# The last projection of an encoder layer: seven block products in place of eight

## Chip, cores and metric

The kernel runs on one core of one Trainium2 chip. The metric is the device time of one launch in microseconds (us); before the change it is 895.59 us, the median of three runs from 895.43 to 895.75.

## What is computed

One layer of an encoder over two groups of 256 tokens with the same weights: a token mixer (retention and latent attention), a residual and a norm, then a gated network of width 2816, a second residual and a norm. The model width is 1024 and everything is float32. What matters here is the last part, cut from the reference:

```python
a, bgate = jnp.split(h @ w_up, 2, axis=-1)
a = _dwconv3(a, conv_w, conv_b)
y = (jax.nn.gelu(a, approximate=False) * bgate) @ w_down
x = _layernorm(DEEPNORM_ALPHA * x + (1.0 + g2) * y) * ln2_g + ln2_b
```

`w_down` is 2816 x 1024. The product `@ w_down` over all 512 tokens, with the residual and norm behind it, is what the change touches. Below, g is what stands left of `@ w_down`.

## The kernel before

**Precision.** A float32 value is held as two parts, hi and lo, in TensorE's 32-bit format. ScalarE (ACT) casts the value to hi (`split_into`, line 148), VectorE (DVE) subtracts hi from the value and writes lo (line 139). A product then costs three matmuls into the same bank, hi by hi, hi by lo and lo by hi (`mm3`, lines 157 to 159). One such matmul takes 128 rows of the inner dimension, 128 tokens and up to 512 columns.

**Storage.** Chunks of weights go through three kinds of buffer of 128 x 2048, each there twice: raw (filled by a DMA from SyncE, SP, line 187), hi and lo. Other things lie in a pool of 69 tiles of 128 x 512. TensorE's sums lie in eight banks of 128 x 512.

**The gated network.** For each of 22 tiles of 128 inner features (index f), TensorE computes two banks `ps_a` and `ps_b` for all 512 tokens; ACT and DVE make the convolution and the gelu of `ps_a` (`up_act`), DVE multiplies with `ps_b`, and the result, the tile `gT[f]` of 128 features by 512 tokens, is split into hi and lo (`g_h`, `g_l`).

**The projection down.** The loop goes over two halves of 512 output columns (c), over chunks of four row tiles of `w_down` (`down_w`, tiles `wd_r`, `wd_h`, `wd_l`), over the row tiles of a chunk, and over four tiles of 128 tokens. In the second half the products of the last 12 row tiles are held back and done token tile by token tile, and the last token tile is done in two pieces of 256 columns. For each finished piece `finish` multiplies by the gate, adds the residual, and takes `bn_stats`; after the second half of a token tile come the mean and variance (`bn_aggr`), two passes over each half of the columns (lines 1194 and 1197), and the two DMAs of the output rows. The power of -1/2 for the norm is on GpSimd (POOL, line 303). The eight residual tiles `x2` come from a scratch in DRAM by DMAs that POOL issues (line 1156).

**Order.** TensorE (PE) runs in the order in which the code is written. The other engines' orders are set by the build's scheduler; each engine then runs its own list strictly in order, and waits at the head of the list on semaphores. A DMA is issued when its issuing engine reaches it in its list. A buffer of a pool is taken again when its last readers are done.

## Time and profile before

| of the profiled execution | |
|---|---|
| span | 893.5 us |
| median of the runs | 895.59 us |
| TensorE busy | 877.2 us, 98% of the span, 4485 matmuls |
| DVE busy | 570.4 us, 64% |
| ACT busy | 354.3 us, 40% |
| POOL busy | 49.8 us, 6% |
| first and last matmul of the projection down start | 764.7 us, 885.4 us |
| mean granted TensorE clock | 0.994 |

The profile is of one execution, whose span runs from its first to its last instruction; 2.1 us of the median lie outside it (895.59 - 893.5). "Busy" of TensorE counts a matmul's whole passage, and passages overlap, so a matmul's cost is the distance from start to start of consecutive ones, not its duration. A row of a group reads: line, engine, operation, out<-in, shapes, count, then busy microseconds, mean nanoseconds of one, and the idle time of the engine before them with what ended it. In a row of the timeline the first number is the start and the second the duration, in us; in a row of a table of windows, the stretch, its length, then each engine's busy time (and number of instructions), the granted TensorE clock, the DMA share and GB/s.

### The profile page before, as it was taken

What the parts mean: (1) busy time and instruction counts of PE and PEld (TensorE: products, weight loads), DVE (VectorE), ACT (ScalarE), POOL (GpSimd) and SP (SyncE); (2) the same over time, 40 slices, a digit from 0 to 9 for tenths busy, and PEclk for the clock granted to TensorE, in tenths of its full rate; (3) what the DMA queues carried; (4) which work ended last, traced back from release to release, by engine and by line L of the source; (5) the groups of instructions that cost most, each with busy time, mean ns of one, the idle gap of its engine ahead of it and who ended that gap; (6) DMA issues with size and microseconds to landing.
All of it is one profiled execution on the core that took longest, in us unless ns stands there. A gap on an engine that the chain in (4) does not pass through costs nothing.

```text
span 893.5 us, 11463 instructions
## 1 busy us (share of the span) xinstructions
PE 877.2 (98%) x4485; PEld 736.5 (82%) x4485; DVE 570.4 (64%) x950; ACT 354.3 (40%) x585; POOL 49.8 (6%) x78
## 2 busy tenths in 40 slices
PE   8999999999999999999998999999999999999996
PEld 5778788888889898988886899888888888888885
DVE  5475877684677777885974966447755755323456
ACT  3555766562343443353342166333333343212200
POOL 3030000000000001000020200000000000100001
PEclk9999999999999999999998999999999999999999
DMA  9922212233545425344356323234334533622401
GB/s 302 388 83 60 70 57 92 67 123 95 153 142 182 113 95 153 131 169 161 111 185 206 111 95 94 60 106 153 119 100 137 160 102 122 208 81 93 142 23 71
DMA packets 118374, 114.29 MB, mean 128 GB/s; under 512 B 6853, under 2 KB 97187, under 8 KB 118320
## 3 DMA queue, kind: packets, MB, share of 16 engines
q1 hardware_dynamic: 114688, 104.00, 35.4%
q0 software_dynamic: 2912, 8.45, 3.3%
...
## 4 chain that ended last, share of the span: by engine, by line
PE 94%; DMA 2%; DVE 1%; ACT 1%; issue 0%; SPq 0%; DVEq 0%; ACTq 0%
PE ps_b L157 5%; PE ps_d L157 5%; PE ps_b L159 5%; PE ps_d L159 5%; PE ps_b L158 5%; PE ps_d L158 4%; PE ps_a L158 4%; PE ps_a L159 4%; PE ps_a L157 4%; PE ps_rv L159 2%; PE ps_rv L158 2%; PE ps_rv L157 2%; PE ps_gb L157 2%; PE ps_ga L157 2%; PE ps_ga L159 2%; PE ps_ga L158 2%
## 5 line engine op out<-in xcount | busy, mean ns | idle before, releaser
L484 DVE SCALAR_TENSOR_TENSOR acc<-araw,csil,acc 128x512 f32<-128x512 f32 x112 | 78.3, 746 | 8.1 <-DMA araw<-in_w_ada_dram 8.1
L157 PE MATMUL ps_b<-h_h,wup_h 128*128 128x512 f32 (+1 forms) x200 | 72.9, 364 | 0.3 <-ACT h2m L394 0.3
L158 PE MATMUL ps_a<-h_l,wup_h 128*128 128x512 f32 (+1 forms) x200 | 73.0, 365 | 0.1
L157 PE MATMUL ps_a<-h_h,wup_h 128*128 128x512 f32 (+1 forms) x200 | 72.8, 364 | 0.0
L159 PE MATMUL ps_b<-h_h,wup_l 128*128 128x512 f32 (+1 forms) x200 | 72.8, 364 | 0.0
L158 PE MATMUL ps_b<-h_l,wup_h 128*128 128x512 f32 (+1 forms) x200 | 72.8, 364 | 0.0
L159 PE MATMUL ps_a<-h_h,wup_l 128*128 128x512 f32 (+1 forms) x200 | 72.8, 364 | 0.0
L158 PE MATMUL ps_d<-wd_l,g_h 128*128 128x512 f32 (+1 forms) x198 | 72.5, 366 | 0.0
L157 PE MATMUL ps_d<-wd_h,g_h 128*128 128x512 f32 (+1 forms) x198 | 72.5, 366 | 0.0
L159 PE MATMUL ps_d<-wd_h,g_l 128*128 128x512 f32 (+1 forms) x198 | 72.4, 366 | 0.0
L148 ACT CAST wup_h<-wup_r 128x1024 fp32r<-128x1024 f32 (+1 forms) x46 | 44.3, 1013 | 49.7 <-PE ps_b L158 36.7
L139 DVE TENSOR_TENSOR wd_l<-wd_r,wd_h 128x1024 fp32r<-128x1024 f32 (+1 forms) x24 | 26.2, 1132 | 58.6 <-ACT wd_h L148 58.4
L139 DVE TENSOR_TENSOR wup_l<-wup_r,wup_h 128x1024 fp32r<-128x1024 f32 (+1 forms) x46 | 52.2, 1174 | 11.3 <-ACT wup_h L148 9.5
L148 ACT CAST wd_h<-wd_r 128x1024 fp32r<-128x1024 f32 (+1 forms) x24 | 22.2, 979 | 73.4 <-PE ps_d L159 69.1
L142 DVE TENSOR_TENSOR conv<-conv,ps_b 128x512 f32<-128x512 f32 x22 | 15.1, 687 | 56.7 <-PE ps_b L159 53.6
L157 PEld LDWEIGHTS ps_b<-h_h,wup_h 128*128 128x128 f32 x200 | 37.8, 189 | 6.4 <-ACT h2m L394 0.5
L158 PEld LDWEIGHTS ps_a<-h_l,wup_h 128*128 128x128 f32 x200 | 37.8, 189 | 6.3 <-DVE h_l L139 0.3
L158 PEld LDWEIGHTS ps_b<-h_l,wup_h 128*128 128x128 f32 x200 | 37.7, 189 | 5.9
L157 PEld LDWEIGHTS ps_a<-h_h,wup_h 128*128 128x128 f32 x200 | 37.7, 189 | 5.9
L159 PEld LDWEIGHTS ps_a<-h_h,wup_l 128*128 128x128 f32 x200 | 37.8, 189 | 5.9
L159 PEld LDWEIGHTS ps_b<-h_h,wup_l 128*128 128x128 f32 x200 | 37.8, 189 | 5.9
L158 PEld LDWEIGHTS ps_d<-wd_l,g_h 128*128 128x128 f32 x198 | 37.4, 189 | 6.1
...
## 6 DMA issues: line engine op xcount, KB each, us to landing
...
araw<-in_w_ada_dram SPq DMA_DIRECT2D x64, 256.0 KB, 5.4
wd_r<-in_w_down_dram SPq DMA_DIRECT2D x10, 1024.0 KB, 4.8
wada<-in_w_ada_dram SPq DMA_DIRECT2D x32, 256.0 KB, 6.0
wga_r<-in_w_in_dram SPq DMA_DIRECT2D x4, 1024.0 KB, 5.0
wmo_r<-in_w_mla_o_dram SPq DMA_DIRECT2D x4, 1024.0 KB, 4.6
...
wrv_r<-in_w_in_dram SPq DMA_DIRECT2D x4, 1024.0 KB, 5.5
```

Of the source, the lines that this page charges most:

```text
L139: (eng or dve).tensor_tensor(out=out, in0=a, in1=b, op=ALU.subtract)
L142: (eng or dve).tensor_tensor(out=out, in0=a, in1=b, op=ALU.mult)
L148: act.copy(hi, src)
L157: pe.matmul(out, l[0], r[0], start=start, stop=False)
L158: pe.matmul(out, l[0], r[1], start=False, stop=False)
L159: pe.matmul(out, l[1], r[0], start=False, stop=stop)
L484: dve.scalar_tensor_tensor(out=acc[g], in0=raw, scalar=s, in1=acc[g], op0=ALU.mult, op1=ALU.add)
```

## The change

The product is cut into blocks: 2 blocks of 256 tokens (the two groups), 2 blocks of 1408 inner features (11 row tiles each), and 2 blocks of 512 columns. The usual scheme takes eight block products; the change takes seven, with sums of blocks on both sides (Strassen's scheme, one level). In the order of the code they are numbered 1, 2, 5, 3, 6, 7, 4. Each is 11 row tiles by two token tiles (s = 0, 1) of 512 columns, three matmuls each, in chunks of 4, 4 and 3 row tiles, and in a chunk all row tiles of s = 0 stand before those of s = 1. Products 1 and 2 share a pair of banks, so do 5 and 3, and so do 7 and 4: product 2 is summed onto product 1 after ACT has copied product 1 out (tiles `dv`; `dw` is the same copy of product 5), and 4 onto 7 after DVE has added 7 to `dw` (in `finish`).

Sums of weights: products 1, 5, 6 and 4 take theirs from 11 tiles `chain_w` (named `wdx` in the rows below), loaded once by SP; after each split of such a tile a DMA from POOL adds the next block of `w_down` to it in place (`accum_op=ALU.add`, line 1218), 33 times 256 KB in all. Products 2, 3 and 7 take raw blocks through the weight buffers (tiles `wdb`); product 7's get a second block added by POOL DMAs in the same way (line 1226: two of 1 MB, one of 0.75 MB). The split parts of the chain are `wdc_h` and `wdc_l`, made 512 columns at a time; those of the blocks are `wdb_h` and `wdb_l`, 1024 at a time.

Sums of g: `gT[f]` stays unsplit. In the gated network the first 11 tiles' first 256 tokens are split for product 1; each of the other 11 tiles brings three subtractions of 128 x 256 on DVE (`g_combine`). In each product the 11 splits of 128 x 256 for the next product are made (`half_split`, ACT and DVE; tiles `ga` and `gs`), in product 1 also 11 more subtractions.

At the end all token tiles are finished in one piece of 512 columns; the two chunks of product 4 that are held back (row tiles 4 to 10) are done for s = 0, then for s = 1.

```diff
-    def mm3(out, l, r, start, stop):
-        pe.matmul(out, l[0], r[0], start=start, stop=False)
...
+    def mm3(out, l, r, start, stop, skip=False):
+        pe.matmul(out, l[0], r[0], start=start, stop=False, skip_group_check=skip)
+        pe.matmul(out, l[0], r[1], start=False, stop=False, skip_group_check=skip)
+        pe.matmul(out, l[1], r[0], start=False, stop=stop, skip_group_check=skip)
...
+        ga11, g_s3 = [], []
+        T1, T2 = slice(0, 256), slice(256, 512)
+        def half_split(src, name, neg=False):
+            w = t512(F32R, name)
+            if neg:
+                act.mul(w[:, T1], src, -1.0)
+                dve.scalar_tensor_tensor(out=w[:, T2], in0=src, scalar=-1.0, in1=as32(w[:, T1]), op0=ALU.mult, op1=ALU.subtract)
+            else:
+                split_into(w[:, T1], w[:, T2], src)
+            return w
+        def g_combine(f):
+            if f < NF2:
+                ga11.append(half_split(gT[f][:, T1], f"ga11_{f}"))
+                return
+            i = f - NF2
+            if i % 2 == 0:
+                g_s3.append(t512(F32, f"gs3_{i}"))
+            lo, hi = gT[i], gT[f]
+            sub(g_s3[i // 2][:, (T1, T2)[i % 2]], lo[:, T2], lo[:, T1])
+            sub(lo[:, T2], lo[:, T2], hi[:, T2])
+            sub(lo[:, T1], lo[:, T1], lo[:, T2])
         def up_act(f, pa, pb):
...
             act.activation(a, a, AF.Gelu)
             mul(a, a, pb)
-            gT[f] = split(a, f"g{f}")
+            gT[f] = a
+            g_combine(f)
...
-        def down_w(c, k0, n, small_tiles=False):
...
-        def finish(t, c, a, b, ps):
...
-        for c in range(2):
...
-            pieces = [(t, 0, 512, ps512(f"ps_d{c}_{t}")) for t in range(4 - c)]
-            if c:
-                pieces += [(3, a, a + 256, ps512(f"ps_d{c}_3_{a}")) for a in (0, 256)]
...
+        def load_x2(t, c):
+            x2[t][c] = t512(F32, f"x2_{t}_{c}")
+            nc.gpsimd.dma_start(x2[t][c], x1d[t * 128:(t + 1) * 128, c * 512:(c + 1) * 512])
+        def stats2(t, c):
+            for m in range(2):
+                n = 2 * c + m
+                dve.bn_stats(out=st2[t][:, 6 * n:6 * n + 6], in_=x2[t][c][:, m * 256:m * 256 + 256])
+        def finish(t, c, ps, more=None):
+            u = t512(F32, f"v{t}_{c}")
+            gate = gates[5, t // 2, c]
+            if more is not None:
+                add(u, more, ps)
+                mul(u, u, gate)
+            else:
+                mul(u, ps, gate)
+            dve.scalar_tensor_tensor(out=x2[t][c], in0=x2[t][c], scalar=ALPHA, in1=u, op0=ALU.mult, op1=ALU.add)
+            stats2(t, c)
+        def norm_out(t):
+            mv = small(2, f"mv2_{t}")
+            dve.bn_aggr(out=mv, in_=st2[t])
+            rs = rstd_of(mv[:, 1:2], LN_EPS, 1, f"ln3_{t}")
+            dst = outs[t // 2][0, (t % 2) * 128:(t % 2) * 128 + 128, :]
+            for cc in range(2):
+                y = x2[t][cc]
+                dve.scalar_tensor_tensor(out=y, in0=y, scalar=mv[:, 0:1], in1=ln2g[cc], op0=ALU.subtract, op1=ALU.mult)
+            for cc in range(2):
+                y = x2[t][cc]
+                dve.scalar_tensor_tensor(out=y, in0=y, scalar=rs, in1=ln2b[cc], op0=ALU.mult, op1=ALU.add)
+                (nc.scalar if cc else nc.sync).dma_start(dst[:, cc * 512:(cc + 1) * 512], y)
+        CHUNKS = [(0, 4), (4, 4), (8, 3)]
+        chain_w = {}
+        def wd_rows(r, c, k0, n=1):
+            return w_down[:, r * NF2 + k0:r * NF2 + k0 + n, c * 512:(c + 1) * 512]
+        def chain_of(more, nxt):
+            def weights(k0, n):
+                hi, lo = w_tiles(f"wdc{k0}")
+                for k in range(k0, k0 + n):
+                    if more is None:
+                        chain_w[k] = t512(F32, f"wdx{k}")
+                        nc.sync.dma_start(chain_w[k], wd_rows(0, 0, k)[:, 0])
+                    cols = slice((k - k0) * 512, (k - k0 + 1) * 512)
+                    split_into(hi[:, cols], lo[:, cols], chain_w[k])
+                    if nxt is not None:
+                        nc.gpsimd.dma_start(chain_w[k], wd_rows(*nxt, k)[:, 0], accum_op=ALU.add)
+                return hi, lo
+            return weights
+        def block_of(r, c, plus=None):
+            def weights(k0, n):
+                raw = w_raw(lambda raw: [(kf(raw, n, 512), wd_rows(r, c, k0, n))], n * 512, f"wdb{r}{c}_{k0}")
+                if plus is not None:
+                    nc.gpsimd.dma_start(kf(raw, n, 512), wd_rows(*plus, k0, n), accum_op=ALU.add)
+                return w_split(raw, n * 512, f"wdb{r}{c}_{k0}")
+            return weights
+        ga = {1: ga11}
+        a_of = {2: lambda i: half_split(gT[NF2 + i][:, T1], f"ga12_{i}"),
+                5: lambda i: half_split(gT[i][:, T2], f"gs1_{i}"),
+                3: lambda i: half_split(gT[NF2 + i][:, T1], f"gs4_{i}"),
+                6: lambda i: half_split(gT[i][:, T1], f"gs2_{i}"),
+                7: lambda i: half_split(g_s3[i // 2][:, (T1, T2)[i % 2]], f"gs3s_{i}"),
+                4: lambda i: half_split(gT[NF2 + i][:, T2], f"ga22_{i}", True)}
+        w_of = {1: chain_of(None, (0, 1)), 2: block_of(1, 0), 5: chain_of(1, (1, 1)), 3: block_of(1, 1),
+                6: chain_of(1, (1, 0)), 7: block_of(1, 1, (0, 1)), 4: chain_of(1, None)}
+        def product(p, nxt, banks, first, last):
+            ga.setdefault(nxt, [])
+            def parts_for_next(k0, n):
+                for i in range(k0, k0 + n) if nxt else ():
+                    ga[nxt].append(a_of[nxt](i))
+                    if nxt == 2:
+                        sub(gT[NF2 + i][:, T1], gT[NF2 + i][:, T1], gT[i][:, T1])
+            def mms(s, k0, n, wc):
+                for k in range(k0, k0 + n):
+                    a = ga[p][k]
+                    mm3(banks[s], (a[:, s * 128:s * 128 + 128], a[:, 256 + s * 128:384 + s * 128]),
+                        cut(wc, slice(None), slice((k - k0) * 512, (k - k0 + 1) * 512)), first and k == 0, k == NF2 - 1, skip=not last or not first)
+            held = []
+            for k0, n in CHUNKS:
+                wc = w_of[p](k0, n)
+                parts_for_next(k0, n)
+                if not nxt and k0:
+                    held.append((k0, n, wc))
+                    for s in range(2):
+                        mms(s, k0, n, wc)
+            if held:
+                for s in range(2):
+                    for h in held:
+                        mms(s, *h)
+                    yield s
+        def banks(name):
+            return [ps512(f"ps_d{name}_{s}") for s in range(2)]
+        b1 = banks(1)
+        drain(product(1, 2, b1, True, False))
+        v = [t512(F32, f"dv{s}") for s in range(2)]
+        for s in range(2):
+            act.copy(v[s], b1[s])
+            load_x2(s, 0)
+        drain(product(2, 5, b1, False, True))
+        for s in range(2):
+            finish(s, 0, b1[s])
+        b5 = banks(5)
+        drain(product(5, 3, b5, True, False))
+        w = [t512(F32, f"dw{s}") for s in range(2)]
+        for s in range(2):
+            act.copy(w[s], b5[s])
+            load_x2(s, 1)
+        drain(product(3, 6, b5, False, True))
+        b6 = banks(6)
+        drain(product(6, 7, b6, True, True))
+        for s in range(2):
+            sub(v[s], b6[s], v[s])
+            add(w[s], v[s], w[s])
+        for s in range(2):
+            finish(s, 1, b5[s], v[s])
+            norm_out(s)
+        for s in range(2):
+            for c in (1, 0):
+                load_x2(2 + s, c)
+        b7 = banks(7)
+        drain(product(7, 4, b7, True, False))
+        for s in range(2):
+            finish(2 + s, 1, b7[s], w[s])
+        for s in range(2):
+            gate = gates[5, 1, 0]
+            mul(v[s], v[s], gate)
+            dve.scalar_tensor_tensor(out=x2[2 + s][0], in0=x2[2 + s][0], scalar=ALPHA, in1=v[s], op0=ALU.mult, op1=ALU.subtract)
+        for s in product(4, None, b7, False, True):
+            u = t512(F32, f"v{2 + s}_0")
+            mul(u, b7[s], gates[5, 1, 0])
+            sub(x2[2 + s][0], x2[2 + s][0], u)
+            stats2(2 + s, 0)
+            norm_out(2 + s)
```

**Order of the instructions at three places.** First DVE from the last tile of the gated network on; `conv_6893` and `conv_6877` are that tile before and in the change. Before:

```order
L1099 SCALAR_TENSOR_TENSOR conv_6893<-ps_a_6843,vecs,conv_6893 128x2x255
L1101 SCALAR_TENSOR_TENSOR conv_6893<-ps_a_6843,vecs,conv_6893 128x2x255
L142 TENSOR_TENSOR conv_6893<-conv_6893,ps_b_6844 128x512
L139 TENSOR_TENSOR wd_4_l<-wd_4_r,wd_4_h 128x1024 x2
L139 TENSOR_TENSOR g_l<-conv_6893,g_h 128x512
L139 TENSOR_TENSOR wd_8_l<-wd_8_r,wd_8_h 128x1024 x2
L139 TENSOR_TENSOR wd_12_l<-wd_12_r,wd_12_h 128x1024 x2
```

In the change the corresponding list, from the third of the subtractions that stand before it to the fourth lo part of product 1's weights (`wdx_6903`, `wdx_6908`, `wdx_6913` and `wdx_6918` are row tiles 0 to 3):

```order
L139 TENSOR_TENSOR conv_6354<-conv_6354,conv_5540 128x256
L139 TENSOR_TENSOR wdc_l<-wdx_6908,wdc_h 128x512
L139 TENSOR_TENSOR ga_4_6985<-conv_6430,ga_4_6985 128x256
L139 TENSOR_TENSOR ga_5_6989<-conv_6507,ga_5_6989 128x256
L142 TENSOR_TENSOR conv_6877<-conv_6877,ps_b_6828 128x512
L139 TENSOR_TENSOR ga_6_6993<-conv_6583,ga_6_6993 128x256
L139 TENSOR_TENSOR ga_7_6997<-conv_6662,ga_7_6997 128x256
L139 TENSOR_TENSOR wdc_l<-wdx_6913,wdc_h 128x512
L139 TENSOR_TENSOR ga_8_7042<-conv_6730,ga_8_7042 128x256
L139 TENSOR_TENSOR conv_6430<-conv_6430,conv_5608 128x256
L139 TENSOR_TENSOR conv_6507<-conv_6507,conv_5676 128x256
L139 TENSOR_TENSOR wdc_l<-wdx_6918,wdc_h 128x512
```

Before, the lo parts of the first chunk stand ahead of this piece and two instructions of 1024 columns follow the multiplication with `ps_b`. Now product 1's lo parts of row tiles 1 to 3 stand between splits of g for product 2 (`ga`) and subtractions.

Second, POOL's list: before, all from the residual tiles on:

```order
L1156 DMA x_0_0_6915<-x1d 128x512
L1156 DMA x_1_0_6917<-x1d 128x512
L1156 DMA x_2_0_6919<-x1d 128x512
L1156 DMA x_3_0_6921<-x1d 128x512
L1156 DMA x_0_1_7257<-x1d 128x512
L1156 DMA x_1_1_7259<-x1d 128x512
L1156 DMA x_2_1_7261<-x1d 128x512
L1156 DMA x_3_1_7263<-x1d 128x512
L303 TENSOR_TENSOR ln_0_rs<-ln_0_ve,half_m 128x1
```

In the change, from the first of product 7's weights on; the rows left out are row tiles 2 to 9 of the same kind:

```order
L1226 DMA wdb_0_r<-in_w_down_dram 128x4x512
L1226 DMA wdb_4_r<-in_w_down_dram 128x4x512
L1218 DMA wdx_6903<-in_w_down_dram 128x512
L1218 DMA wdx_6908<-in_w_down_dram 128x512
...
L1218 DMA wdx_7037<-in_w_down_dram 128x512
L1164 DMA x_2_1_7664<-x1d 128x512
L1164 DMA x_2_0_7666<-x1d 128x512
L1164 DMA x_3_1_7668<-x1d 128x512
L1164 DMA x_3_0_7670<-x1d 128x512
L1226 DMA wdb_8_r<-in_w_down_dram 128x3x512
L303 TENSOR_TENSOR ln_0_rs<-ln_0_ve,half_m 128x1
```

The DMA that adds to product 7's last chunk (`wdb_8`, row tiles 8 to 10) stands behind those for `wdb_0` and `wdb_4`, the eleven that make product 4's weights, and four residual tiles.

Third, DVE where one pair of banks passes to the next product. Before, at the change from the first to the second half of the columns, which have banks of their own:

```order
L139 TENSOR_TENSOR wd_20_l<-wd_20_r,wd_20_h 128x1024
L139 TENSOR_TENSOR wd_0_l<-wd_0_r,wd_0_h 128x1024 x2
L142 TENSOR_TENSOR v_0_0_7237<-ps_d_0_6923,ada_0_0_6221 128x512
L142 TENSOR_TENSOR v_0_0_7242<-ps_d_1_6924,ada_0_0_6221 128x512
L1148 SCALAR_TENSOR_TENSOR x_0_0_6915<-x_0_0_6915,v_0_0_7237 128x512
L142 TENSOR_TENSOR v_0_0_7247<-ps_d_2_6925,ada_0_1_6226 128x512
L1148 SCALAR_TENSOR_TENSOR x_1_0_6917<-x_1_0_6917,v_0_0_7242 128x512
L142 TENSOR_TENSOR v_0_0_7252<-ps_d_3_6926,ada_0_1_6226 128x512
L1151 BN_STATS st_0_6911<-x_0_0_6915 128x6 x2
```

In the change, behind the lo parts of product 7's last chunk; `ps_d_0_7672` is the bank of s = 0 that product 7 leaves to product 4, and the last row is the one that reads it:

```order
L1180 SCALAR_TENSOR_TENSOR x_1_1_7359<-x_1_1_7359,v_1_7646 128x512
L139 TENSOR_TENSOR wdc_l<-wdx_6903,wdc_h 128x512
L1309 SCALAR_TENSOR_TENSOR x_3_0_7670<-x_3_0_7670,dv_7073 128x512
L139 TENSOR_TENSOR wdc_l<-wdx_6908,wdc_h 128x512
L1185 BN_AGGR mv_0_7634<-st_0_6895 128x2
L139 TENSOR_TENSOR wdc_l<-wdx_6913,wdc_h 128x512
L139 TENSOR_TENSOR wdc_l<-wdx_6918,wdc_h 128x512
L1169 BN_STATS st_1_6896<-x_1_1_7359 128x6 x2
L302 TENSOR_SCALAR ln_0_ve<-mv_0_7634 128x1
L1190 SCALAR_TENSOR_TENSOR x_0_0_7075<-x_0_0_7075,mv_0_7634,ln2g_6887 128x512
L1190 SCALAR_TENSOR_TENSOR x_0_1_7356<-x_0_1_7356,mv_0_7634,ln2g_6889 128x512
L145 TENSOR_TENSOR v_1_7800<-dw_7353,ps_d_0_7672 128x512
```

Two residual passes, four lo parts of product 4's weights, the sums of two token tiles and the first two passes of a norm stand ahead of that addition.

55 lines of the change are left out of this document (1 added, 54 removed).

## The prediction

> **What bounds the kernel now.** I read the engine shares first, then the chain of work that ended last, then the projection's own instructions.
>
> ```profile
> PE 877.2 (98%) x4485; PEld 736.5 (82%) x4485; DVE 570.4 (64%) x950; ACT 354.3 (40%) x585; POOL 49.8 (6%) x78
> ...
> PE 94%; DMA 2%; DVE 1%; ACT 1%; issue 0%; SPq 0%; DVEq 0%; ACTq 0%
> ```
>
> TensorE is busy nearly throughout and is 94% of the chain: before the change a matmul saved is time saved. Next the projection down, by windows (the fourth ends with the last matmul) and by two of its three groups of matmuls, then the distance between matmuls on its timeline.
>
> ```profile
> core 0: us, PE busy (x) PEld busy (x) DVE busy (x) ACT busy (x) POOL busy (x), PEclk, DMA share, GB/s
> 764.70:794.90 30.20, 30.20 (x135) 24.98 (x135) 8.37 (x8) 6.54 (x7) 0.35 (x1) 1.00 0.40 132
> ...
> 855.30:885.70 30.40, 30.35 (x168) 26.43 (x166) 17.41 (x35) 0.00 (x0) 2.83 (x3) 1.00 0.14 52
> 885.70:893.50 7.80, 0.00 (x0) 0.00 (x0) 4.33 (x9) 0.00 (x0) 0.98 (x1) 0.79 0.17 67
> sum 128.80, PE 120.95 PEld 102.52 DVE 53.53 ACT 20.75 POOL 4.17; mean PE 24.19 PEld 20.50 DVE 10.71 ACT 4.15 POOL 0.83
> ```
> ```profile
> L157 PE MATMUL ps_d<-wd_h,g_h x198: 277/389/397, 764.7 to 885.1; 128*128 128x512 f32 x154, 128*128 128x256 f32 x44
> ...
> L159 PE MATMUL ps_d<-wd_h,g_l x198: 278/389/390, 765.2 to 885.4; 128*128 128x512 f32 x154, 128*128 128x256 f32 x44
> ```
> ```profile
> 829.63 0.28 PE L159 MATMUL ps_d<-wd_h,g_l 128*128 128x256 f32 x1
> 829.75 0.28 PE L157 MATMUL ps_d<-wd_h,g_h 128*128 128x256 f32 x1
> ...
> 870.74 0.39 PE L157 MATMUL ps_d<-wd_h,g_h 128*128 128x512 f32 x1
> 870.97 0.39 PE L158 MATMUL ps_d<-wd_l,g_h 128*128 128x512 f32 x1
> 871.19 0.39 PE L159 MATMUL ps_d<-wd_h,g_l 128*128 128x512 f32 x1
> 871.42 0.39 PE L157 MATMUL ps_d<-wd_h,g_h 128*128 128x512 f32 x1
> ```
>
> The projection takes 120.95 us of TensorE with no gap, DVE is busy for 53.53 us of it, and 7.8 us follow the last matmul. A 512-wide matmul costs (871.42 - 870.74) / 3 = 0.227 us, a 256-wide one 0.12. There are 3 x 154 = 462 and 3 x 44 = 132: 104.9 + 15.8 = 120.7, as measured.
>
> **TensorE's saving.** Seven products of 11 x 2 x 3 = 66 matmuls are 462 of 512 columns: 104.9 us. That is **-15.8 us**, if it never waits.
>
> **DVE's new work.** Its prices:
>
> ```profile
> L139 DVE TENSOR_TENSOR wd_l<-wd_r,wd_h 128x1024 fp32r<-128x1024 f32 x18 | 21.4, 1222 | 58.5 <-ACT wd_h L148 58.4
> L1194 DVE SCALAR_TENSOR_TENSOR x<-x,mv,ln2g 128x512 f32<-128x512 f32 x8 | 5.6, 744 | 0.0
> L139 DVE TENSOR_TENSOR wd_l<-wd_r,wd_h 128x512 fp32r<-128x512 f32 x4 | 2.5, 684 | 0.0
> ```
> ```profile
> L139 DVE TENSOR_TENSOR h_l<-h2m,h_h 128x256 fp32r<-128x256 f32 x16 | 6.1, 418 | 7.8 <-ACT h_h L395 7.8
> ```
> ```profile
> 880.99 0.74 DVE L1197 SCALAR_TENSOR_TENSOR x<-x,ln_rs,ln2b 128x512 f32<-128x512 f32 x1
> 881.65 0.42 DVE L142 TENSOR_TENSOR v<-ps_d,ada 128x256 f32<-128x256 f32 x1
> 881.99 0.74 DVE L1197 SCALAR_TENSOR_TENSOR x<-x,ln_rs,ln2b 128x512 f32<-128x512 f32 x1
> 882.65 0.42 DVE L1148 SCALAR_TENSOR_TENSOR x<-x,v 128x256 f32<-128x256 f32 x1
> ...
> 885.69 0.42 DVE L142 TENSOR_TENSOR v<-ps_d,ada 128x256 f32<-128x256 f32 x1 [2.16 <-PE ps_d L159]
> 886.14 0.43 DVE L1148 SCALAR_TENSOR_TENSOR x<-x,v 128x256 f32<-128x256 f32 x1
> 886.61 0.43 DVE L1151 BATCH_NORM_STATS2 st<-x 128x6 f32<-128x256 f32 x1
> 887.07 0.26 DVE L1189 BATCH_NORM_AGGREGATE mv<-st 128x2 f32<-128x24 f32 x1
> ```
>
> Independent instructions start 0.08 us before the last one's duration is over (880.99 to 881.65 is 0.66 for 0.74). So in a queue a 1024-wide split costs 1.14, a 512-wide one 0.60, a pass (scalar_tensor_tensor) 0.66, a 256-wide operation 0.34 (a pass of 256, no row of its form, 0.37), `bn_stats` 0.34. During the seven products DVE gets 44 splits of the chain (26.4), three times five of 1024 and one of 512 (18.9), 66 of g (22.8), 11 subtractions (3.7), 20 multiplications and additions of 512 (12.0), 20 passes (13.2), 14 `bn_stats` (4.8) and trifles: about 103 us, **against 104.9 of TensorE**. Twice the 53.5 of before, in a list of fixed order: any place where the order is bad stalls TensorE. I followed the list at each first use:
>
> 1. Product 1's start.
>
> ```profile
> 759.50 0.78 ACT L1097 ACTIVATE conv<-ps_a,vecs 128x512 f32<-128x512 f32 x1 [3.15 <-PE ps_a L159]
> ```
> ```profile
> 760.31 0.75 DVE L1099 SCALAR_TENSOR_TENSOR conv<-ps_a,vecs,conv 128x510 f32<-128x510 f32 x1 [2.43 <-ACT conv L1097]
> 761.09 0.75 DVE L1101 SCALAR_TENSOR_TENSOR conv<-ps_a,vecs,conv 128x510 f32<-128x510 f32 x1
> ```
>
> DVE is through these passes at 761.8. Seven 256-wide operations (2.4) and the lo part of row tile 0 (0.6) end at 764.8, when product 1 begins (764.7 before). Row tile 1's follows in time. Row tile 2's is behind two splits of g, the 512-wide multiplication, two more splits: 0.34 x 4 + 0.60 x 2 = 2.6, done 3.6 us after the start; TensorE gets there at 1.7. Wait 1.9. Row tile 3's needs 3 x 0.34 + 0.6 = 1.6 more, TensorE 0.7. Wait 0.9. Sum **2.9 us**.
>
> 2. Product 7's third chunk. The bank of product 6's s = 0 is complete 9 x 0.227 = 2.0 us before product 7 starts, 0.4 later DVE subtracts. From there its list holds ten 512-wide operations (6.0), three 1024-wide splits (3.4), 11 splits of g with a sign (4.1), two passes (1.3), two `bn_stats` (0.7) and the lo part of row tiles 8 and 9 itself (1.2): 16.7, done 15.1 us into product 7. TensorE wants it after 48 matmuls and one, 11.1. Wait **4.0 us**.
>
> 3. Product 4's first matmul into the bank of s = 0. The addition that frees it stands behind the rows shown last in the section on the change: 7.2 us of DVE after row tiles 8 and 9. TensorE has 17 matmuls left then, 3.9. Wait **3.3 us**.
>
> 4. Row tiles 8 and 9 of product 4: after that addition 9.7 us of DVE, against 36 matmuls and one, 8.4; then 1.3 against 0.7. Wait **1.8 us**.
>
> Together 12.0 us; nothing else on the list comes later than its use. ACT covers its own share (each cast is shorter than the DVE operation that follows it); in the gated network 33 subtractions and 11 splits of 256 columns (15.0) replace 22 lo parts of 512 (13.2), under TensorE's work.
>
> **The tail.** Before, from the last bank: 885.69 to 887.07 is 1.4 us up to `bn_aggr`. Now the multiplication is 512 wide (0.60), a pass of the token tile before it stands next (0.66), then the subtraction (0.72 with its dependence), two `bn_stats` (0.34 + 0.46): 2.8. With 0.1 for the wider last matmul, **+1.5 us**; the rest of the tail stays.
>
> If the accumulating DMAs were free, the sum would be -15.8 + 12.0 + 1.5 = -2.3 us.
>
> **The accumulating DMAs.** The trace has none. Its plain ones:
>
> ```profile
> wd_r<-in_w_down_dram SPq DMA_DIRECT2D x10, 1024.0 KB, 4.8
> ...
> x<-x1d POOLq DMA_DIRECT2D x8, 256.0 KB, 5.2
> ```
> ```profile
> 470.00:474.00 4.00, 4.00 (x19) 3.13 (x17) 0.00 (x0) 0.00 (x0) 0.00 (x0) 1.00 1.04 396
> ```
>
> All engines busy move 396 GB/s. Lower bound: an accumulating DMA as a plain one, since it must at least bring in the block. Upper bound: three plain ones (read the block, read the tile, write the tile). I take twice a plain one: both operands have to be fetched, the writing runs beside the fetching in a plain one too. The Trainium skill ("Collectives: The Full Stack", section "The bandwidth ceiling: the fold count and why AG ≠ RS ≠ AR") gives half the rate for a sum of two sources against a copy, 31 against 62 GB/s, because both sources are read on one ring; no run here shows it, and the sum by it is the one below.
>
> Where does it reach the path? The sums for products 5, 6 and 4 have a product or more of time each. The tight place is POOL's list at product 7: `wdb_0`, `wdb_4`, eleven tiles, four residual tiles, then `wdb_8`. The raw buffer for `wdb_0` is free when product 3's second chunk is split, wanted 44.9 + 2.9 + 5.4 = 53.2 us into the products; its load takes 4.8 and the issue some more, so the first sum starts at 58.5. Up to `wdb_8`'s landing 2 + 2.75 + 0.75 = 5.5 MB are summed (11 MB at twice the price), 1 MB of residuals and 1.75 MB of raw blocks loaded: 13.75 x 1.049 MB at 390 GB/s is 37 us. So 95.5, some 2 us for the landing, 1.05 for the cast: 98.5. Product 7's third chunk is wanted at 5 x 14.97 + 2.9 + 10.9 = 88.7. TensorE waits about 9.5, and 1.0 more for the lo part: 10.5 in place of point 2's 4.0. Points 3 and 4 stay, since DVE waits at the same row. **Sum: -15.8 + 2.9 + 10.5 + 3.3 + 1.8 + 1.5 = +4.2 us.** Against the profiled execution 893.5 + 4.2 = 897.7 of span; the median has 2.1 us more: **899.8 us**.
>
> **Rivals.**
> A. *The sums cost little more than plain DMAs*: up to about 1.55 times, they land before DVE wants them, and the order of DVE decides: 895.6 - 2.3 = **893.3 us**. For it: the DMA share of 0.40 and 0.14 in the projection's first and last window leaves much spare.
> B. *The sums cost three plain ones* (slower still): 16.5 + 2.75 = 19.25 MB, 51.8 us, landing at 112.3 + 1.05; the wait is 25.5 and the sum +19.2: **915 us**. By this reckoning the kernel loses from 1.7 times on, where the wait passes 6.3 us.
> C. *TensorE stays the bound*: DVE's list keeps ahead by some slack that I missed and only the saving and the tail count: 895.6 - 14.3 = **881.3 us**. Against it: DVE's 103 us for 104.9, and instructions that wait at the head of a strict list.
> D. *A long wait also halves TensorE's clock.*
>
> ```profile
> 474.00:477.20 3.20, 0.18 (x1) 0.00 (x0) 0.52 (x1) 1.59 (x3) 0.00 (x0) 1.00 0.15 54
> 477.20:480.30 3.10, 2.44 (x4) 1.12 (x4) 3.10 (x5) 2.48 (x4) 0.00 (x0) 0.50 0.00 0
> 480.30:484.02 3.72, 3.72 (x9) 2.95 (x10) 1.75 (x3) 0.00 (x0) 0.00 (x0) 0.50 0.88 254
> ```
>
> Once, 3.0 us without matmuls were followed by 6.8 us at half clock, worth 3.4 us of full work. After a 10 us wait the same follows; of it DVE's next wait (point 3) hides most, since TensorE would reach that bank 3.3 us early. At most 3.4 more after it: **903 us**. The Trainium skill ("TensorE: Matmul & The Clock Gate", "What's actually happening") puts the window at about 3.4 us of idleness; the trace agrees with its half clock, at 0.50, and shows it after 3.0.
>
> **How the numbers follow.** Forecast (about twice) 0.41, A 0.25, B 0.17, D 0.11, C 0.06. What this kernel's measurement can tell from no change is 0.2%, 1.8 us. Faster by that: C and three quarters of A, 0.25; same: the rest of A and the forecast's lower edge (1.6 to 1.8 times), 0.14; slower 0.61. The likeliest's own range is 896 to 903 (1.75 to 2.2 times). The range to hold 8 in 10 leaves out C and the far half of B: 892 to 915.
>
> **What would show it.** Right: TensorE's longest wait lies before product 7's 49th matmul, ended by ACT's cast of `wdb_8`, itself by a POOL DMA; DVE near 100 us in the products; waits of 2 to 4 us at the start and at the bank of product 4. An accumulating tile of 256 KB then shows a rate near half of 396 GB/s when they queue. Wrong: DVE, not a DMA, ends that wait (A); waits on accumulated tiles at products 5 or 6 as well (B); no waits over 1 us (C). A list of DVE that I mistimed by 2 us would shift the forecast by as much.

## The result and the profile after

The change makes the kernel slower: 901.39 us median (901.32 to 902.67) against 895.67 (895.43 to 896.64), a ratio of 1.0064 with an interval of 1.0050 to 1.0078, or 5.7 us. The forecast was 899.8, in a range from 892 to 915, with slower at 0.61. The profiled execution has a span of 899.6, 6.1 more than before.

The engine shares of after, its chain of waits by engine, and the queue of the DMAs that POOL issues (packets, megabytes, share of 16 DMA engines):

```profile
PE 866.6 (96%) x4353; PEld 722.2 (80%) x4353; DVE 623.4 (69%) x1097; ACT 386.9 (43%) x682; POOL 83.1 (9%) x114
...
q0 software_dynamic: 9120, 19.99, 10.8%
...
PE 87%; DVE 5%; DMA 4%; ACT 2%; issue 1%; SPq 0%; DVEq 0%; ACTq 0%; POOLq 0%
```

The chain was TensorE to 94%; it is now 87%, and DVE, DMAs and ACT have what it lost. TensorE's timeline of after, its first and last matmul of the projection down and three in between:

```profile
765.83 0.39 PE L157 MATMUL ps_d<-wdc_h,ga 128*128 128x512 f32 x1
...
864.95 0.79 PE L157 MATMUL ps_d<-wdb_h,gs3s 128*128 128x512 f32 x1 [10.20 <-ACT wdb_h L148]
...
867.22 0.63 PE L157 MATMUL ps_d<-wdb_h,gs3s 128*128 128x512 f32 x1
867.65 0.63 PE L158 MATMUL ps_d<-wdb_l,gs3s 128*128 128x512 f32 x1
...
889.82 0.39 PE L159 MATMUL ps_d<-wdc_h,ga 128*128 128x512 f32 x1
```

From the first start to the end of the last slot (889.82 + 0.23) are 124.2 us, for 462 matmuls that need 104.9. Most of the 19.3 us between is in four groups of TensorE's waits in the projection (engine, tile and line, what it waited for; us in all, times, longest):

```profile
PE ps_d L157 <- ACT wdb_h L148: 10.2, 1, 10.2
PE ps_d L158 <- DVE wdc_l L139: 3.3, 4, 1.6
PE ps_d L157 <- DVE v L145: 0.5, 1, 0.5
PE ps_d L158 <- DVE wdb_l L139: 0.5, 1, 0.5
```

These are 14.5 us of idleness; the rest is matmuls that restart late or at half clock (867.22 to 867.65 is 0.43 a matmul, against 0.227). The long wait followed back, in the chain of waits of after (start, duration, what):

```profile
842.74 1.15 DVE wdb_l L139
843.90 11.62 DMA wdb_r<-in_w_down_dram
855.58 0.52 issue
856.10 7.65 DMA wdb_r<-in_w_down_dram
...
863.85 1.05 ACT wdb_h L148
```

DVE's split of `wdb_0` frees the raw buffer at 843.9; SP loads the 0.75 MB of `wdb_8` in 11.6 us; only then can POOL issue its sum, which needs 7.7 us; then ACT casts, and TensorE starts at 864.95. The stretches around it, of after (busy time of each engine, granted clock, DMA share, GB/s):

```profile
842.00:853.00 11.00, 11.00 (x50) 9.10 (x49) 11.00 (x20) 5.39 (x13) 4.87 (x7) 1.00 1.11 229
853.00:864.00 11.00, 1.75 (x8) 1.13 (x6) 4.20 (x10) 0.15 (x1) 1.31 (x1) 0.71 0.93 216
864.00:875.00 11.00, 9.04 (x26) 6.59 (x27) 10.07 (x19) 5.68 (x10) 1.00 (x1) 0.67 0.03 9
...
sum 134.90, PE 110.97 PEld 88.67 DVE 106.10 ACT 60.09 POOL 41.20; mean PE 11.10 PEld 8.87 DVE 10.61 ACT 6.01 POOL 4.12
```

While the load and the sum run, the DMA engines are full (1.11 and 0.93) and move 216 to 229 GB/s; the plain row of before had 396 at 1.04. DVE, busy for only 4.2 us from 853 to 864, has 106.1 us of work between 764.7 and the end of the span.

### The profile page after: what moved, and what is told of

Read it like the earlier page. It is cut to its first block, busy times and chain, and to the rows that moved or that the text cites. A ratio compares the mean times of both kernels' runs of the same rounds, so it can differ in the third digit from the quotient of the medians.

```text
span 899.6 us, 11589 instructions
## 1 busy us (share of the span) xinstructions
PE 866.6 (96%) x4353; PEld 722.2 (80%) x4353; DVE 623.4 (69%) x1097; ACT 386.9 (43%) x682; POOL 83.1 (9%) x114
## 3 DMA queue, kind: packets, MB, share of 16 engines
q0 software_dynamic: 9120, 19.99, 10.8%
q10 hardware_dynamic: 720, 1.11, 0.3%
## 4 chain that ended last, share of the span: by engine, by line
PE 87%; DVE 5%; DMA 4%; ACT 2%; issue 1%; SPq 0%; DVEq 0%; ACTq 0%; POOLq 0%
PE ps_a L158 4%; PE ps_a L159 4%; PE ps_a L157 4%; PE ps_b L157 4%; PE ps_b L158 4%; PE ps_b L159 4%; PE ps_d L158 3%; PE ps_d L159 3%; PE ps_d L157 3%; DMA wdb_r<-in_w_down_dram 2%; PE ps_rv L159 2%; PE ps_rv L158 2%; PE ps_rv L157 2%; PE ps_gb L157 2%; PE ps_ga L157 2%; PE ps_ga L158 2%
## 5 line engine op out<-in xcount | busy, mean ns | idle before, releaser
L1124 ACT ACTIVATE conv<-ps_a,vecs 128x512 f32<-128x512 f32 x22 | 17.2, 780 | 71.1 <-PE ps_a L159 71.1
L1218 POOL DMA_DIRECT2D wdx<-in_w_down_dram x33 | 29.5, 1233 | 73.2 <-DVE wdc_l L139 64.4
L159 PE MATMUL ps_rv<-wrv_h,h_l 128*128 128x256 f32 x128 | 36.2, 283 | 0.0
L158 PE MATMUL ps_rv<-wrv_l,h_h 128*128 128x256 f32 x128 | 36.2, 283 | 0.0
L157 PE MATMUL ps_rv<-wrv_h,h_h 128*128 128x256 f32 x128 | 36.2, 283 | 0.0
L1126 DVE SCALAR_TENSOR_TENSOR conv<-ps_a,vecs,conv 128x510 f32<-128x510 f32 x22 | 16.4, 747 | 28.3 <-ACT conv L1124 28.2
```

Of the source, the lines that this page charges most:

```text
L157: pe.matmul(out, l[0], r[0], start=start, stop=False, skip_group_check=skip)
L158: pe.matmul(out, l[0], r[1], start=False, stop=False, skip_group_check=skip)
L159: pe.matmul(out, l[1], r[0], start=False, stop=stop, skip_group_check=skip)
L1124: act.activation(a, pa, AF.Identity, scale=convw[:, 1, f:f + 1], bias=convb[:, f:f + 1])
L1126: dve.scalar_tensor_tensor(out=av_[:, :, 1:256], in0=pv[:, :, 0:255], scalar=convw[:, 0, f:f + 1], in1=av_[:, :, 1:256], op0=ALU.mult, op1 ...
L1218: nc.gpsimd.dma_start(chain_w[k], wd_rows(*nxt, k)[:, 0], accum_op=ALU.add)
```

## The experiments

Each kernel is compared with the kernel before, whose median was 895.5 to 896.1 beside them. The table divides the span of each profiled execution into four, all read from the timeline: the start of the first matmul of the projection down, the stage from there to 0.23 us after the start of the last matmul (its slot; the same is taken for before, where the last one is 256 wide), from there to the end of DVE's last pass, and the closing behind that. The four add up to the span.

| kernel | median us | ratio, interval | first | stage | to DVE's end | closing |
|---|---|---|---|---|---|---|
| before | 895.67 | | 764.7 | 120.9 | 4.6 | 3.3 |
| after | 901.39 | 1.0064, 1.0050 to 1.0078 | 765.8 | 124.2 | 6.2 | 3.3 |
| plain DMAs | 896.50 | 1.0011, 1.0002 to 1.0020 | 765.7 | 117.9 | 6.3 | 5.9 |
| no sums for product 7 | 896.18 | 1.0005, 0.9997 to 1.0014 | 766.0 | 116.0 | 8.0 | 5.7 |
| no sums for product 4 | 895.95 | 1.0007, 0.9998 to 1.0016 | 764.8 | 118.6 | 6.2 | 5.0 |
| TensorE kept busy | 902.45 | 1.0076, 1.0064 to 1.0089 | 765.2 | 124.9 | 6.1 | 3.3 |
| early weights | 898.65 | 1.0039, 1.0027 to 1.0051 | 764.3 | 124.4 | 6.6 | 3.3 |
| own tiles | 896.87 | 1.0015, 1.0006 to 1.0023 | 766.6 | 118.2 | 7.6 | 3.4 |
| both | 895.22 | 1.0000, 0.9989 to 1.0011 | 765.2 | 117.3 | 6.8 | 3.4 |
| both, fewer passes | 894.39 | 0.9988, 0.9979 to 0.9997 | 764.5 | 120.6 | 6.0 | 3.4 |
| plain, fewer passes | 893.04 | 0.9972, 0.9962 to 0.9981 | 764.3 | 114.8 | 6.0 | 5.9 |
| both, lo parts on GpSimd | 895.88 | 1.0001, 0.9991 to 1.0012 | 765.2 | 119.8 | 5.6 | 3.4 |
| light, plain | 885.77 | 0.9889, 0.9876 to 0.9903 | 766.4 | 105.9 | 6.0 | 6.1 |
| light, with sums | 892.71 | 0.9964, 0.9952 to 0.9976 | 765.1 | 117.3 | 6.0 | 3.4 |

Two columns need a word first. "First" varies by 2.3 us among kernels that share everything ahead of it but the position of a few instructions, so the 1.1 us that it is later in after are not shown to be the change's. "Closing" is 3.3 or 3.4 in some kernels and 5.0 to 6.1 in others, and differences of the medians hold that too; it is taken up at the end of this part. What tests the theories is the stage, with two limits. The profiled executions lie from 1.2 us below (TensorE kept busy) to 2.0 us above (both, fewer passes) the median of their kernel, so a difference of stages under some 2 us says little by itself. And DVE's list is that of after, instruction for instruction, only with plain DMAs and without the sums for product 4; in the other kernels the scheduler orders it anew in places.

**What the accumulating DMAs cost.** The first kernel takes the adding away and keeps every DMA; the next two leave out some of the sums whole.

```diff
-                        nc.gpsimd.dma_start(chain_w[k], wd_rows(*nxt, k)[:, 0], accum_op=ALU.add)
+                        nc.gpsimd.dma_start(chain_w[k], wd_rows(*nxt, k)[:, 0])
...
-                    nc.gpsimd.dma_start(kf(raw, n, 512), wd_rows(*plus, k0, n), accum_op=ALU.add)
+                    nc.gpsimd.dma_start(kf(raw, n, 512), wd_rows(*plus, k0, n))
```

> All 36 accumulating DMAs become plain ones of the same size, at the same places of every engine's list; left out is the adding, so the tiles hold the last block alone. Theory (the sums cost about twice a plain DMA and this decides product 7's last chunk): TensorE's wait there falls from 10.7 us to the 3 to 4 us that VectorE's list alone asks for, full clock stays or is lost only briefly, and the time falls from 901.4 to 893 to 895 us. Rival (the two transfers in series, load and then sum, are too late at any price): the wait stays at 7 us or more, the time at 898 or above.

The queue's share and the issues (KB each, median us to landing), first of plain DMAs, then of after:

```profile
q0 software_dynamic: 6304, 19.99, 7.1%
...
wdx<-in_w_down_dram POOLq DMA_DIRECT2D x33, 256.0 KB, 3.7
...
wdb_r<-in_w_down_dram POOLq DMA_DIRECT2D x1, 768.0 KB, 4.5
```
```profile
wdx<-in_w_down_dram POOLq DMA_DIRECT2D x33, 256.0 KB, 7.2
...
wdb_r<-in_w_down_dram POOLq DMA_DIRECT2D x1, 768.0 KB, 7.6
```

Both move 19.99 MB; the queue's other DMAs, those of before, have 3.3%. So the additions make a DMA (10.8 - 3.3) / (7.1 - 3.3) = **1.97 times** as long for the DMA engines: the forecast took 2. The shares of the other kernels with all additions (10.8 to 11.0%) and with plain DMAs alone (7.1 to 7.4%) put it between 1.8 and 2.0. The Trainium skill ("Collectives: The Full Stack", section "The bandwidth ceiling: the fold count and why AG ≠ RS ≠ AR") gives half the rate for a sum of two sources; the trace agrees, at 1.97. On TensorE, timeline, waits and windows of plain DMAs, and last the first window of after:

```profile
765.69 0.39 PE L157 MATMUL ps_d<-wdc_h,ga 128*128 128x512 f32 x1
...
883.34 0.39 PE L159 MATMUL ps_d<-wdc_h,ga 128*128 128x512 f32 x1
```
```profile
PE ps_d L158 <- DVE wdb_l L139: 3.2, 1, 3.2
PE ps_d L157 <- ACT wdc_h L148: 1.3, 1, 1.3
```
```profile
764.70:782.00 17.30, 15.07 (x58) 11.27 (x57) 13.55 (x31) 6.91 (x15) 6.95 (x13) 0.90 0.74 244
...
853.00:864.00 11.00, 7.81 (x28) 5.85 (x27) 11.00 (x24) 3.65 (x6) 0.00 (x0) 0.84 0.13 52
864.00:875.00 11.00, 9.71 (x43) 7.72 (x42) 11.00 (x23) 3.84 (x7) 1.92 (x2) 1.00 0.13 49
```
```profile
764.70:782.00 17.30, 15.09 (x64) 11.51 (x63) 14.51 (x32) 8.52 (x17) 10.74 (x13) 1.00 1.01 196
```

The long wait is gone and 3.2 us for DVE's lo part stand at its place, with DVE busy for 22.00 of 22 us. The stage is 6.3 us shorter and the closing 2.6 longer; the median falls by 4.9 us and misses what was expected by 1.5. Without the longer closing it would be 893.9, an estimate, and within it. The stage, 117.9, is near rival A's sum for free additions, 104.9 + 12.0 = 116.9, but not by the same parts. Behind point 1's two waits the clock falls to half here (0.90 in the first window, where after has 1.00 behind the same waits), which costs some 1.6 us; behind the wait for the lo part it falls again (0.84 in the window from 853), some 1.7 us; and the wait at the bank of product 4, point 3, is 1.3 us where the sum has 3.3. That the totals agree to 1.0 is partly luck.

```diff
-                6: chain_of(1, (1, 0)), 7: block_of(1, 1, (0, 1)), 4: chain_of(1, None)}
+                6: chain_of(1, (1, 0)), 7: block_of(1, 1), 4: chain_of(1, None)}
```

> Product 7 uses its raw blocks: its three accumulating DMAs are left out (and with them the second block). The eleven sums for product 4 and all others stay. Theory: the wait of 10.7 us is made of the crowded load of the last chunk (12 us where 5 are usual) and of its own sum (7.6 us), so without the sum it falls to 3 to 4 us, where VectorE's list takes over: 893 to 895.5 us. Rival (the traffic of the eleven sums alone decides): the wait falls by less than 3 us, the time stays above 898.

The wait is 2.1 us, for DVE's lo part. TensorE ends its stage early, but DVE is 1.8 us further behind by then than in after (8.0 against 6.2), and the closing is 2.4 us longer: the time is 0.7 us above what was expected, the wait below it.

```diff
-                6: chain_of(1, (1, 0)), 7: block_of(1, 1, (0, 1)), 4: chain_of(1, None)}
+                6: chain_of(1, None), 7: block_of(1, 1, (0, 1)), 4: chain_of(1, None)}
```

> The eleven sums that make product 4's weights are left out (product 4 takes the tiles as product 6 left them); product 7's three sums stay. Theory: the load of product 7's last chunk takes about 5 us again instead of 12, its sum still 5 to 8: the wait falls from 10.7 to about 4 us, the time to 894 to 896 us. Rival (load and sum in series behind a late buffer, whatever else runs): the wait stays at 7 us or more, the time at 898 or above.

POOL's timeline, TensorE's waits and SP's timeline of this kernel, in which the sum for `wdb_8` stays and the eleven ahead of it go:

```profile
849.44 1.30 POOL L1226 DMA_DIRECT2D wdb_r<-in_w_down_dram  x1 [15.79 <-DMA wdb_r<-in_w_down_dram]
```
```profile
PE ps_d L157 <- ACT wdb_h L148: 2.9, 1, 2.9
```

```profile
844.51 0.37 SPq L187 DMA_DIRECT2D wdb_r<-in_w_down_dram  x1
```

SP issues the load (the last row) as late as in after (843.90), and 4.9 us later POOL issues the sum; in after this took 12.2. So the eleven sums cost the path some 7 us by crowding a plain load; the sum of `wdb_8` behind it takes 7.7 us in both kernels. The time is as expected. Taking either half away brings the wait down to 2 or 3 us. Here load and sum still end it, but DVE is through its list only 0.5 us earlier.

**Whether the half clock costs anything (rival D).** 40 unread matmuls of 512 columns into a free bank fill the wait:

```diff
+                    if p == 7 and k0 == 8:
+                        fill = ps512("ps_fill")
+                        for _ in range(40):
+                            pe.matmul(fill, ones, wide, start=True, stop=True)
```

> Forty products of 512 columns that nothing reads (9.1 us at full clock) stand on TensorE ahead of product 7's last chunk, into a bank that is free; nothing else is changed. They fill the long wait, so the clock should stay at 1.00 after it. Theory (behind the wait VectorE's list decides, so the half clock of about 7 us was mostly hidden): the wait for the bank of product 4 grows from 0.5 to 3 or 4 us and the time falls by 1 to 2 us, to 899.5 to 900.5. Rival (the half clock is on the path): the time falls by 4 to 5 us, to 896.5 to 897.5.

The same stretch behind the wait in both, after first, and then the next wait of the kernel that was kept busy:

```profile
864.60:869.00 4.40, 3.59 (x8) 2.50 (x9) 4.07 (x6) 2.89 (x6) 0.00 (x0) 0.50 0.00 0
```
```profile
864.60:869.00 4.40, 3.64 (x16) 2.84 (x16) 4.40 (x8) 2.28 (x5) 0.00 (x0) 1.00 0.00 0
```
```profile
PE ps_d L157 <- DVE v L145: 3.7, 1, 3.7
```

The clock is 1.00 instead of 0.50 and 16 matmuls are done instead of 8, but the wait for the bank of product 4 (point 3) grows from 0.5 to 3.7, and behind that wait the clock falls all the same. Two matmuls there, on this kernel's timeline, 0.43 us apart:

```profile
874.04 0.63 PE L159 MATMUL ps_d<-wdc_h,ga 128*128 128x512 f32 x1
874.47 0.63 PE L157 MATMUL ps_d<-wdc_h,ga 128*128 128x512 f32 x1
```

So the half clock is moved rather than removed, and the time lies above both expectations. Nor is DVE's list quite the same: one more pass stands ahead of the addition that frees the bank, which starts 8.3 us after the lo part of `wdb_8` here and 7.5 us in after. What shows that the half clock behind the long wait costs nothing is after itself: with its matmuls at half clock TensorE still comes 0.5 us too early to the bank, so DVE sets the time there.

**The waits at the start and before product 7's last chunk.** The first chunk of product 1 is cast and split before the last tile of the gated network:

```diff
+            if f == NF - 1:
+                firsts.append(chain_of(None, (0, 1))(0, 4))
...
-                wc = w_of[p](k0, n)
+                wc = firsts.pop() if p == 1 and not k0 else w_of[p](k0, n)
```

> Product 1's first four weight tiles are written ahead of the last tile of the gated network, so VectorE makes their lo parts before it; the rest is as in the change. The two waits at product 1's start (1.6 and 0.6 us) should vanish. Theory (product 7's late chunk hangs behind TensorE's own progress, since its buffer comes free with product 6): all that follows moves forward, the time falls by 2 to 3 us, to 898.5 to 899.5. Rival (the queue of sums runs by its own clock): the long wait grows by what the start saves, the time stays within 0.7 us of 901.4.

The two waits of 1.6 and 0.6 us are gone, and the median falls by 2.7 us against after, as expected. The trace does not show that this is why. TensorE has other waits in product 1 instead, the longest 0.9 us, so that its delays there (what its starts lie apart beyond 0.227 us a matmul) add up to 2.5 us where after has 3.1; and the long wait has grown, as the rival has it:

```profile
PE ps_d L157 <- ACT wdb_h L148: 11.6, 1, 11.6
```

The stage is 124.4. This execution took 900.37 us, 1.7 above the median; where the others gain is open.

Then product 7's last chunk in three tiles of its own, loaded and summed during product 3:

```diff
+        def own_load():
+            for k in range(8, NF2):
+                own.append(t512(F32, f"wdo{k}"))
+                nc.sync.dma_start(own[-1], wd_rows(1, 1, k)[:, 0])
+                nc.gpsimd.dma_start(own[-1], wd_rows(0, 1, k)[:, 0], accum_op=ALU.add)
...
-                wc = w_of[p](k0, n)
+                wc = own_split() if p == 7 and k0 == 8 else w_of[p](k0, n)
```

> Product 7's last chunk gets three tiles of its own, loaded and summed during product 3 instead of behind product 6; all is still computed. The wait of 10.7 us should fall to 2 or less and the clock stay full. Theory (behind that wait VectorE's list is the bound): the freed time reappears as a wait for the bank of product 4 and as a later end of VectorE, so that the time is that of the plain DMAs or a little less, 895 to 897 us. Rival (the wait was the only loss): 901.4 - 10.7 - about 2 of slow clock, below 890 us.

```profile
PE ps_d L157 <- DVE v L145: 3.0, 1, 3.0
PE ps_d L158 <- DVE wdo_l L139: 1.9, 2, 1.7
```

These waits of own tiles stand where after has 10.2 and 0.5. All that after sums is still summed (in 38 DMAs, since the last chunk's is cut in three), and 4.5 us come back, as expected: what hurt was the place of one sum, with its load, in front of a deadline. Both edits together:

> Both edits together: product 1's first weights early, and own tiles for product 7's last chunk; all is still computed. Theory (VectorE's list): the start's 2.5 us come on top of the own tiles' gain, 892.5 to 894.5 us, which is 1 to 3 us under the kernel before. Rival (gains at different places of one list swallow each other): no better than the own tiles alone by more than 0.7 us.

The ratio is 1.0000: no slower than before, and no faster. It misses what was expected by 0.7 us, and at 1.7 us under own tiles alone it is better than the rival. The stage, 117.3, is only 0.9 shorter than with own tiles alone: TensorE's delays in product 1 fall from 3.0 to 1.7 us, but those in products 7 and 4 are 10.8 us where they were 10.3, a wait of 3.5 us for a lo part of product 4 among them.

**Whether DVE is the bound behind the sums.** Two kernels leave out work that DVE does during the products: the two normalizing passes of the first two token tiles, eight operations of 512 columns.

```diff
-                dve.scalar_tensor_tensor(out=y, in0=y, scalar=mv[:, 0:1], in1=ln2g[cc], op0=ALU.subtract, op1=ALU.mult)
+                if t > 1:
+                    dve.scalar_tensor_tensor(out=y, in0=y, scalar=mv[:, 0:1], in1=ln2g[cc], op0=ALU.subtract, op1=ALU.mult)
```

> As with both edits, but the first two token tiles are written out without the norm's two passes: left out are eight passes of 512 columns, 8 x 0.66 = 5.3 us of VectorE in products 7 and 4, nothing of TensorE or of the loads. Theory (VectorE's list bounds the last two products): 3 to 4.5 us faster than both edits alone, 888.5 to 891. Rival (TensorE or a DMA bounds them): within 0.7 us of it.

> Plain DMAs in place of the sums, as in the first experiment (the adding is left out), and besides the first two token tiles are written out without the norm's two passes (left out: eight passes of 512 columns, 5.3 us of VectorE in products 7 and 4). No DMA is late here, so VectorE alone is tested. Theory (VectorE's list bounds the last two products and the end): 3 to 4.5 us faster than the plain DMAs alone, 892 to 893.5. Rival (TensorE or DMAs bound them): within 0.7 us of 896.5.

On plain DMAs it gains 3.5 us of 896.5, as expected, by a stage of 114.8 instead of 117.9; TensorE's delays in product 4 fall from 3.2 to 0.2 us. On the kernel with both edits it gains 0.8 instead of the 3 or more expected. This run decides nothing on DVE: its profiled execution took 896.39 us, 2.0 above the median, and in it something else came up. DVE's timeline and TensorE's waits there:

```profile
862.49 0.69 DVE L1331 SCALAR_TENSOR_TENSOR x<-x,dv 128x512 f32<-128x512 f32 x1 [3.12 <-DMA x<-x1d]
```
```profile
PE ps_d L157 <- DVE v L145: 5.9, 1, 5.9
```

DVE, ahead of its time now, stands 3.1 us for a residual tile: its DMA is on POOL behind the sums. In after the same wait is 3.3 us, under the long wait of TensorE.

Next, seven lo parts of product 4 go from DVE to GpSimd (the engine of the row POOL):

```diff
-                    split_into(hi[:, cols], lo[:, cols], chain_w[k])
+                    split_into(hi[:, cols], lo[:, cols], chain_w[k], pool if nxt is None and k > 3 else None)
```

> Both edits (first weights early, own tiles for product 7's last chunk), and the lo parts of product 4's last seven row tiles are subtracted on GpSimd instead of VectorE (7 x 0.60 = 4.2 us off VectorE's list); all is still computed. GpSimd has issued its last DMA by then and is idle; no row shows its price for 128 x 512. Theory (VectorE's list is the bound, and GpSimd needs less than about 1.3 us each): 891 to 893, below the kernel before by 2.5 to 4.5. Rival (GpSimd needs 2 us or more each, or slows VectorE meanwhile): TensorE waits for GpSimd in product 4, no faster than both edits alone, 894.5 or above.

The group on GpSimd, and a pass of DVE in this kernel and, below, in the one with both edits:

```profile
L139 POOL TENSOR_TENSOR wdc_l<-wdx,wdc_h 128x512 fp32r<-128x512 f32 x7 | 11.5, 1672 | 9.2 <-ACT wdc_h L148 9.2
```
```profile
L1218 DVE SCALAR_TENSOR_TENSOR x<-x,ln_rs,ln2b 128x512 f32<-128x512 f32 x8 | 7.6, 986 | 0.0
```
```profile
L1218 DVE SCALAR_TENSOR_TENSOR x<-x,ln_rs,ln2b 128x512 f32<-128x512 f32 x8 | 5.6, 739 | 0.0
```

GpSimd takes 1672 ns where DVE takes some 680, and DVE's pass slows from 739 to 986. No gain, as the rival had it. The Trainium skill ("SBUF — State Buffer", section "Who interferes with whom") has DVE and GpSimd share a port by an exclusive lock; the trace agrees: the groups of DVE that slow down have both inputs in SBUF (this one, its like at line 1215 from 741 to 862, a multiplication from 681 to 921), while `bn_stats`, with one, stays at 413 and 412.

At last DVE is made light: both edits, no passes for the first two token tiles, and no lo parts of g (TensorE does all 462 matmuls, with hi in lo's place); once with plain DMAs and once with the sums.

```diff
-                split_into(w[:, T1], w[:, T2], src)
+                act.copy(w[:, T1], src)
...
-                    mm3(banks[s], (a[:, s * 128:s * 128 + 128], a[:, 256 + s * 128:384 + s * 128]),
+                    mm3(banks[s], (a[:, s * 128:s * 128 + 128], a[:, s * 128:s * 128 + 128]),
```

> What is left when both VectorE and the DMAs are relieved: plain DMAs in place of the sums, first weights early, own tiles for product 7's last chunk, no norm passes for the first two token tiles, and no lo parts of g made in the seven products (TensorE takes the hi part in the lo part's place); left out are the adding, 8 passes and 77 lo parts of 128 x 256. TensorE still does all 462 matmuls. Theory (TensorE's saving of 15.8 us is there and only VectorE and the sums take it): no wait over 2 us in the products, 882 to 884.5 us, against 881.3 of the case in which TensorE stays the bound. Rival (the block products cost TensorE more than their count says, by banks shared or by weights): 888 or above.

> As the one before, but with the accumulating DMAs (all 36, of the same size, with the adding). VectorE is as light, so what the sums cost by themselves is seen. Theory (twice the price of a plain DMA fills the DMA engines from product 1 to 7, so product 7's weights are late even in tiles of their own): waits of 5 to 9 us for product 7's weights, 889 to 893 us. Rival (only the late third chunk was the trouble, and VectorE hides the rest): within 1.5 us of the plain DMAs, below 886.

The same window of both, plain first:

```profile
842.00:857.00 15.00, 14.30 (x64) 11.50 (x62) 15.00 (x27) 9.24 (x22) 0.00 (x0) 1.00 0.10 37
```
```profile
842.00:857.00 15.00, 10.31 (x38) 7.80 (x37) 7.45 (x11) 6.21 (x15) 3.89 (x6) 0.89 1.12 220
```

With plain DMAs the stage is 105.9 us, for 104.9 of matmuls: TensorE's saving of 15.8 us is there to the microsecond (120.9 - 105.9 = 15.0) once neither DVE nor a DMA holds it up. The median missed what was expected by 1.3 us; the first matmul is 1.6 later than before and the closing 2.8 longer. With the sums the time is as expected and the stage 117.3, 11.4 more. Of that 8.2 are in product 7: the DMA engines are full (1.12) and TensorE waits, now for the second chunk (3.9 us), and runs at half clock behind the wait. Another 2.5 are in product 1.

**The closing.** Each engine ends with a drain, and in these traces the span ends only when all are over. POOL's and SP's drains in after, then with plain DMAs (ns min/median/max, first and last start; POOL's longest is its first, SP's short one follows the landing of the output):

```profile
L1337 POOLq DRAIN  x3: 46/93/5027, 893.7 to 899.3; - x3
L1337 SPq DRAIN  x3: 7/7/7, 898.8 to 899.1; - x3
```
```profile
L1337 POOLq DRAIN  x3: 46/98/7722, 887.2 to 895.5; - x3
...
L1337 SPq DRAIN  x3: 7/7/7, 892.3 to 895.2; - x3
```

In after POOL's drain is over at 893.7 + 5.0 = 898.7, just as SP has seen the output land; with plain DMAs at 894.9, 2.6 us after SP. It is a property of the kernel, not of an execution: the two kernels with plain DMAs and the same 6304 packets both have 7.72, the three with all sums and 9120 packets 5.03. What sets its length is open. It is 5.0 to 5.2 in all kernels with all the sums, 4.8 before, 6.8 to 7.9 where sums were taken away, and it follows neither the number of POOL's DMAs nor that of packets alone (2912, 6304, 9120 packets: 4.78, 7.72, 5.03). Between kernels whose packets differ little it grows by 5.1 to 5.2 ns a packet (6304 to 6336: 7.72 to 7.89; 7536 to 7664: 6.83 to 7.48; 9120 to 9152: 5.03 to 5.19), as a count would that starts anew on the way; that is not shown, and no run was made on it.

No kernel that computes the whole layer beats the one before; with both edits it ties, with or without GpSimd.

## Why the prediction was right

It was right in the sign, the place and nearly the size: +5.7 us measured, +4.2 forecast. Some of that agreement is luck. By its steps:

- **TensorE's saving, -15.8.** Right. The light kernel shows it, at 15.0 with one wait left.
- **DVE near its limit.** Right: 103 us forecast for the products, 98.9 measured in the stage (106.1 counted to the span's end), and full occupation wherever the DMAs let go (plain DMAs, 853 to 875). Free sums leave a stage of 117.9 against the 116.9 of the forecast's four points, with half clock in place of most of point 3.
- **The price of a sum, twice a plain DMA.** Right, 1.97, with 216 to 229 GB/s where the engines are full, near half of 396. But the price does not decide the sign, as the forecast had it: by its reckoning the kernel gains up to 1.7 times a plain DMA, and at 1.0, with plain DMAs, it gained nothing (896.50 us, a ratio of 1.0011). The sums account for 4.9 of the 5.7 us.
- **The long wait, 10.5.** Right in place and size: 10.2 of idleness and some 11.4 from start to start, with the lo part. (Its own figures, 98.5 less 88.7, make the wait 9.8 and not 9.5; the forecast would have been +4.5.) The bytes queued up to `wdb_8` over the rate put its landing at 97.5 us into the products, and it landed at 97.9 (856.10 + 7.65 - 765.83), with the DMA engines full from 827 to 856. Yet that working is only a part of what happened. By the bytes alone `wdb_8` would land 14.8 us earlier without the eleven sums (5.5 x 1.049 MB at 390 GB/s); without them it landed 5.7 earlier, 92.3 us into the products (849.44 + 7.65 - 764.83). The trace shows a chain in series behind a late buffer: a load of 11.6 us that wants 4.3 where the eleven sums are gone, and 7.7 us for the sum. That the two reckonings end at nearly the same time is luck.
- **Points 1, 3 and 4: 2.9, 3.3 and 1.8.** Measured from start to start: 3.1 us in product 1, 2.5 of it at the two waits; 0.7 at the bank behind some 2.5 of half clock; 1.8 in the rest of product 4, 1.4 of it at two waits. Rival D's mechanism ran as written: the half clock used up the time that TensorE would have waited at point 3, 3.2 us together where 3.3 was forecast. Behind the long wait it therefore costs nothing. It is not free everywhere: with plain DMAs the half clock in product 1 cost some 1.6 us.
- **The tail, +1.5.** Measured 9.8 from the last matmul's start to the end against 8.1 before: 1.7.
- **What the sum lacked.** The stage grew by 3.4 (120.86 to 124.22) against -15.8 + 18.5 = 2.7: the terms of the waits were 0.7 too small together. The first matmul is 1.1 late, which no term had, and which the runs don't put down to the change. With 0.1 of the tail this is the 1.9 that the span's growth of 6.1 has over 4.2.
- **Rival A, 893.3 for sums at little more than a plain DMA.** Its mechanism is that of the kernel with plain DMAs, which took 896.5. The stage came out 1.0 above its sum, with 1.6 of half clock in product 1 that the sum lacks; most of the rest is the closing, 2.6, that no trace shown before had. Without that it would have been near 894, an estimate from the two drains.
